# Attention scores, value sums and norm of a mixer laid out by feature tile

## The chip, the cores and the metric

The kernel runs on one core of a Trainium2 chip. The metric is the device time in microseconds (us) of one execution. Three runs of the kernel before gave a median of 1655.06 us (1654.47 to 1655.62). In the text PE is the matrix engine, DVE the vector engine, ACT the scalar engine, POOL is GpSimd and SP issues the weight transfers.

## The reference

One token block of 256 positions with 1024 features goes through a feed-forward layer, a hybrid mixer, a cross-attention, a second feed-forward layer and then a second block. All is fp32. The change lies in the hybrid mixer, in the part that the reference calls stick-breaking attention (16 heads of 64 features) and in the RMS norm of its result:

```python
z = jnp.einsum('bhtd,bhsd->bhts', qb, kb) * scale
causal = s_idx[None, :] < t_idx[:, None]
log_1mb = jnp.where(causal, jax.nn.log_sigmoid(-z), 0.0)
suffix = lax.cumsum(log_1mb, axis=3, reverse=True) - log_1mb
log_a = jnp.where(causal, jax.nn.log_sigmoid(z) + suffix, -jnp.inf)
a = jnp.exp(log_a)
outs.append(jnp.einsum('bhts,bhsd->bhtd', a, vb))
...
o_att = rmsnorm(o_att, attn_norm_g)          # over the 1024 features of a token
...
return jnp.concatenate([o_att, o_ssd], axis=-1) @ w_out
```

So each head needs scores, a masked exponential of running sums, a product with the values, and then one mean of squares over all 16 heads for each token.

## The kernel before, in words

Weights stream from HBM in units of 128 x 1024 fp32. For each unit SP loads one of three `raw` buffers, ACT rounds it to `hi` (L169), and DVE computes the remainder `lo = raw - hi` (L170). The next load into a `raw` buffer waits for the L170 that read it last. PE multiplies `hi` and `lo` with the activations, which stand in the same two parts (`uT`, `memT`), in three products. `f_tile` (L324) makes one tile of 128 output features by 256 tokens from one unit, 24 matmuls into one of two accumulators `mm`; an `evac` then copies the accumulator to SBUF, and the tile after the next can't start before that copy is done. `half_chunk` (L286) does the same token-major from four units.

Work that is not a weight product is written as Python generators ("sides"). `tick` is called at places in these loops with an estimate of time passed, and steps the sides that are due; a side yields the time after which it wants to go on. So the program order on each engine is fixed when the kernel is built, and each engine runs its instructions in that order, waiting on semaphores.

In the mixer, 8 pairs of f_tiles make `qT` and `kT` (feature-major: 128 features, two heads, to a tile). Two attention sides (`par` 0 and 1) run beside these and beside the 12 convolution tiles (`xs`, `bc`). A step of a side does two heads from two neighbouring feature tiles, both on the same 64 rows: scores (L612, L614), mask (L616, L617), ACT and DVE work, running sums (L634, L635, L637), exponentials and the product with the values (L647 to L649), whose result `oat` is token-major. There are 8 steps.

After the convolution tiles come the `z` product (two chunks of two halves, `half_chunk`), then 8 f_tiles `mk`, whose evacuation is a DVE copy (L933). The side `chain` (L898) is stepped within `z` and `mk`: squares of `oat` with row sums on ACT, `halves_rstd` (a DVE sum and a power of -1/2 on POOL, L438, for one column), the activation of the convolution result (L904), the scaling of `oat` on DVE (L910), and 16 PE transposes (L410 in `transposes`) that bring it feature-major into `oT`, rounded by ACT (L415) and DVE (L419) into two parts, with the gain per feature.

Of the kernel before, what the change touches and what calls it, by code (L numbers as in the profile page):

```python
# [5 lines left out]
F32 = mybir.dt.float32  # L6
# [5 lines left out]
AF = mybir.ActivationFunctionType  # L12
OP = mybir.AluOpType
# [3 lines left out]
EPS = 1e-6  # L17
# [43 lines left out]
COL = {}  # L61
# [55 lines left out]
class Builder:  # L117
# [475 lines left out]
    AW = (0.94, 1.2, 4.0, 4.0, 3.21)  # L593
    A0 = 12.35

    def attention(self, par, qT, kT, vt, oat, ready):

        nc = self.nc
        rows = slice(par * 64, par * 64 + 64)
        A, B = self.acc[2 * par], self.acc[2 * par + 1]  # L600
        z0, z1, o = A, B[:, 0:256], B[:, 256:512]
        zv, z1v = A.rearrange("p (n t) -> p n t", n=2), z1.rearrange("p (n t) -> p n t", n=2)
        ov = o.rearrange("p (t n c) -> p t n c", t=2, n=2)
        neg = self.neg_le[:, None, :].to_broadcast([128, 2, 128])
        oview = oat.rearrange("p t (j n q c) -> p t j n q c", j=4, n=2, q=2)
        opt = dict(skip_group_check=True)
        for j in range(4):
            while ready[0] <= j:
                yield
            for n in range(2):  # L610
                f = 2 * j + n
                nc.tensor.matmul(zv[:, n], kT[rows, f, 0:128], qT[rows, f, :], start=(n == 0), stop=False,  # L612
                                 **opt)
                nc.tensor.matmul(z1v[:, n], kT[rows, f, 128:256], qT[rows, f, 128:256], start=(n == 0),  # L614
                                 stop=False, **opt)
            nc.tensor.matmul(zv[:, :, 0:128], self.ident_bf, neg, start=False, stop=False, **opt)  # L616
            nc.tensor.matmul(z1v, self.ident_bf, neg, start=False, stop=False, **opt)  # L617
            sp = self.FA.alloc(768)
            s0, s1 = sp.ap[:, 0:512], sp.ap[:, 512:768]
            nc.scalar.activation(s0, z0, AF.Abs)  # L620
            nc.scalar.activation(s1, z1, AF.Abs)
            yield self.AW[0]
            nc.scalar.activation(sp.ap, sp.ap, AF.Exp, scale=-1.0)
            nc.scalar.activation(sp.ap, sp.ap, AF.Ln, bias=1.0)
            yield self.AW[1]
            nc.vector.scalar_tensor_tensor(s0, z0, 0.0, s0, op0=OP.max, op1=OP.add)
            nc.vector.scalar_tensor_tensor(s1, z1, 0.0, s1, op0=OP.max, op1=OP.add)
            ph, pl = self.RA.alloc(768), self.RA.alloc(768)
            nc.scalar.activation(ph.ap, sp.ap, AF.Copy)
            nc.vector.tensor_sub(pl.ap, sp.ap, ph.ap.bitcast(F32))  # L630
            yield self.AW[2]
            for p in (ph, pl):
                x0, x1 = p.ap[:, 0:512], p.ap[:, 512:768]
                nc.tensor.matmul(z0, self.ntri, x0, start=False, stop=False, **opt)  # L634
                nc.tensor.matmul(zv[:, :, 128:256], self.none, x1.rearrange("p (n t) -> p n t", n=2),  # L635
                                 start=False, stop=False, **opt)
                nc.tensor.matmul(z1, self.ntri, x1, start=False, stop=(p is pl), **opt)  # L637
            nc.scalar.activation(s0, z0, AF.Exp)
            nc.scalar.activation(s1, z1, AF.Exp)
            ph.free()  # L640
            pl.free()
            yield self.AW[3]
            for n in range(2):
                h = 4 * j + 2 * n + par
                vh = slice(h * 64, h * 64 + 64)
                a0, a1 = s0[:, n * 256:n * 256 + 256], s1[:, n * 128:n * 128 + 128]
                nc.tensor.matmul(ov[:, 0, n], a0[:, 0:128], vt[:, 0, vh], start=(n == 0), stop=False, **opt)  # L647
                nc.tensor.matmul(ov[:, 1, n], a0[:, 128:256], vt[:, 0, vh], start=False, stop=False, **opt)
                nc.tensor.matmul(ov[:, 1, n], a1, vt[:, 1, vh], start=False, stop=(n == 1), **opt)  # L649
            for n in range(2):  # L650
                nc.vector.tensor_copy(oview[:, :, j, n, par, :], ov[:, :, n])
            sp.free()
            yield self.AW[4]
        ready[1] += 1

# [181 lines left out]
    def mixer(self, before_t1, done, mid):  # L837
        nc, F, uT = self.nc, self.FA, self.uT
# [4 lines left out]
        vt = vb.v(t=2, d=1024)  # L843
# [2 lines left out]
            return lambda t, ps: nc.scalar.activation(vt[:, t, c * 512:c * 512 + 512], ps, AF.Copy)  # L846
        self.opening(FIRST["v"], uT, [evv(0), evv(1)], before_t1)
        mblocks, memT = self.tpair(8)
        qb, kb, ob = (F.alloc(2048) for _ in range(3))
        qT, kT, oat = qb.v(f=8, t=256), kb.v(f=8, t=256), ob.v(t=2, d=1024)  # L850
        nc.scalar.preload_act_table_set("natural_log_exp_and_others")
        self.add_side(self.mem_prep(memb, memT), 0.15)
        ready = [0, 0]
        for par in range(2):
            self.add_side(self.attention(par, qT, kT, vt, oat, ready), 0.2)[2] = par * self.A0
        for f in range(8):
            self.f_tile(FIRST["qk"] + 2 * f, uT,
                        lambda ps: nc.scalar.activation(qT[:, f], ps, AF.Copy, scale=0.125))
# [31 lines left out]
        oblocks, oT = self.tpair(8)  # L890
        kmb, zb = F.alloc(2048), F.alloc(2048)
        kmT, zt = kmb.v(f=8, t=256), zb.v(t=2, d=1024)
        ready = [0, 0, 0]
# [2 lines left out]
            return lambda t, ps: nc.scalar.activation(zt[:, t, c * 512:c * 512 + 512], ps, AF.Copy)  # L896

        def chain():  # L898
            rs = []
            for t in range(2):  # L900
                rs.append(self.halves_rstd(self.x_ss(oat[:, t])))
                yield 5.0
            for f in range(12):
                nc.scalar.activation(xp[:, f, 3:259], xp[:, f, 3:259], AF.Silu,  # L904
                                     bias=self.cols[:, COL["conv_b"] + f:COL["conv_b"] + f + 1])
                if f % 2:
                    yield 2.5
                if f in (3, 5):
                    t = f // 2 - 1
                    nc.vector.tensor_scalar(oat[:, t], oat[:, t], rs[t], None, op0=OP.mult)  # L910
                if f > 7:
                    n = f - 8
                    self.transposes(oat[:, n // 2], n // 2, oT, COL["attn_norm_g"], part=n % 2)
                    yield 0.3
            ob.free()
            ready[1] = 1
            nc.scalar.preload_act_table_set("natural_log_exp_and_others")
            yield from self.ssd(xp, zt, uT, ready)

        def gate():  # L920
# [4 lines left out]
            yield  # L925
        row = self.load_row("mix_post_g")
        self.add_side(chain(), 1.41)
        for c in range(2):
            self.tok_chunk(FIRST["z"] + 4 * c, uT, evz(c))
# [881 lines left out]
```

## Time and profile before

| what | value |
|---|---|
| profiled execution | 1655.53 us |
| its span in the trace | 1653.8 us |
| median of three runs | 1655.06 us |
| PE busy | 1632.5 us (99%) |
| DVE busy | 1148.0 us (69%) |
| ACT busy | 977.9 us (59%) |
| POOL busy | 268.6 us (16%) |

A busy time is the union of an engine's instructions. The profiled execution is 0.47 us above the median, and 1.7 us of it lie outside the span. In a timeline a row stands for one instruction or for several neighbours of one kind ("x2"), with its start and length in us; where the engine sat idle before it, brackets tell how long and what ended that. The chip runs an fp32 matmul as two passes, so one call of the program shows as two instructions; a matmul on fp32r operands is one. Matmuls overlap in their ends, so the cost of one in a dense stretch is the distance between starts, not its length.

### The profile page before, as it was taken

The page shows a single profiled execution, that of the slowest core. Times are in us where ns is not written, and L with a number is a line of the kernel's source. Part 1 is how long each engine was busy: PE and PEld are TensorE (multiplying, and loading weights), DVE is VectorE, ACT ScalarE, POOL GpSimd, SP SyncE. Part 2 cuts the span into 40 slices and gives each one's busy share as a digit, 9 for nine tenths or more (in the row PEclk, how much of TensorE's full clock was granted, in tenths as well). Part 3 has the DMA queues.
Part 4 walks back from the last instruction along what each step waited for, and adds up shares of the span by engine and source line. Part 5 has one row for each costly group of instructions (what it writes and reads, how often), then busy time and mean ns, then how long its engine had stood idle before and what let it go on. Part 6 is the DMA issues. An engine that isn't in the chain of part 4 may idle for free.

```text
span 1653.8 us, 29236 instructions
## 1 busy us (share of the span) xinstructions
PE 1632.5 (99%) x11102; PEld 1481.6 (90%) x11102; DVE 1148.0 (69%) x2366; ACT 977.9 (59%) x1826; POOL 268.6 (16%) x311
## 2 busy tenths in 40 slices
PE   8999999999999999999999999999999999999998
PEld 6999899988898899979889999999999888888886
DVE  6554765877756645487657998899999755555554
ACT  6443676786555544467355565888877555444454
POOL 0000000000000000000100003988888000000000
PEclk9999999999999999999999999999999999999999
DMA  7565643364524656555244555444454555555553
GB/s 280 192 208 175 227 143 116 115 202 143 179 103 154 216 190 206 177 185 197 78 140 143 192 190 192 166 163 164 161 166 153 180 205 194 194 195 193 191 191 128
DMA packets 79325, 288.77 MB, mean 175 GB/s; under 512 B 8784, under 2 KB 8912, under 8 KB 79056
## 3 DMA queue, kind: packets, MB, share of 16 engines
q1 hardware_dynamic: 77904, 281.66, 49.8%
q10 hardware_dynamic: 1280, 5.24, 1.0%
q8 instruction: 87, 1.43, 0.3%
q14 instruction: 54, 0.44, 0.1%
HBM read 285.82 MB, written 1.05 MB: 173 GB/s over the span
## 4 chain that ended last, share of the span: by engine, by line
PE 81%; DVE 11%; ACT 3%; issue 2%; DMA 2%; POOL 1%; SPq 0%; POOLq 0%; DVEq 0%; ACTq 0%
PE mm L332 12%; PE mm L334 12%; PE mm L333 12%; PE acc L349 10%; PE acc L351 10%; PE acc L353 10%; DVE lo L170 4%; PE mm L303 2%; PE mm L300 2%; PE mm L299 2%; DMA raw<-ws 2%; PE sd L1388 1%; ACT hi L169 1%; DVE m L1378 1%; DVE X L1260 1%
## 5 line engine op out<-in xcount | busy, mean ns | idle before, releaser
L170 DVE TENSOR_TENSOR lo<-raw,hi 128x1024 fp32r<-128x1024 f32 x414 | 506.6, 1228 | 237.5 <-ACT hi L169 236.1
L332 PE MATMUL mm<-uT,hi 128*128 128x256 f32 x2104 | 597.1, 284 | 2.1 <-DVE X L1491 1.7
L334 PE MATMUL mm<-uT,lo 128*128 128x256 f32 x2104 | 587.1, 279 | 0.0
L333 PE MATMUL mm<-uT,hi 128*128 128x256 f32 x2104 | 586.9, 279 | 0.0
L169 ACT ACTIVATE hi<-raw 128x1024 fp32r<-128x1024 f32 x414 | 436.3, 1058 | 214.9 <-PE acc L353 171.1
L332 PEld LDWEIGHTS mm<-uT,hi 128*128 128x128 f32 x2104 | 397.1, 189 | 4.9 <-DVE X L1491 2.6
L333 PEld LDWEIGHTS mm<-uT,hi 128*128 128x128 f32 x2104 | 397.1, 189 | 0.8
L334 PEld LDWEIGHTS mm<-uT,lo 128*128 128x128 f32 x2104 | 397.0, 189 | 0.0
L1375 POOL TENSOR_SCALAR m<-iota,kT 128x128 f16<-128x128 f16 x256 | 233.2, 927 | 197.8 <-DVE kT L1358 149.9
L438 POOL TENSOR_TENSOR hr<-hv,mhalf 128x1 f32<-128x1 f32 x26 | 14.4, 552 | 816.3 <-DVE hv L437 816.3
L349 PE MATMUL acc<-hi,wf 128*128 128x512 f32 x384 | 118.9, 390 | 0.0
L351 PE MATMUL acc<-lo,wf 128*128 128x512 f32 x384 | 118.7, 389 | 0.0
L353 PE MATMUL acc<-hi,wf 128*128 128x512 f32 x384 | 118.5, 389 | 0.0
L170 DVE TENSOR_TENSOR lo<-fa,hi 128x1024 fp32r<-128x1024 f32 x69 | 84.1, 1233 | 34.0 <-ACT hi L169 33.7
L531 ACT ACTIVATE fa<-mm 128x256 f32<-128x256 f32 x36 | 13.8, 383 | 122.9 <-PE mm L334 122.9
L351 PEld LDWEIGHTS acc<-lo,wf 128*128 128x128 f32 x384 | 72.1, 188 | 15.2
L353 PEld LDWEIGHTS acc<-hi,wf 128*128 128x128 f32 x384 | 72.1, 188 | 15.1
L349 PEld LDWEIGHTS acc<-hi,wf 128*128 128x128 f32 x384 | 72.1, 188 | 14.9
L1488 ACT ACTIVATE X<-mm 128x256 f32<-128x256 f32 (+40 forms) x126 | 39.6, 314 | 76.0 <-PE mm L334 75.0
L1377 ACT ACTIVATE oh<-m,kT 128x128 f16<-128x128 f16 x256 | 81.1, 390 | 0.0
L169 ACT ACTIVATE hi<-fa 128x1024 fp32r<-128x1024 f32 x69 | 70.7, 1051 | 5.6 <-PE mm L303 3.1
L1398 DVE TENSOR_TENSOR X<-sd,X 128x184 f32<-128x184 f32 (+31 forms) x64 | 60.9, 951 | 1.2 <-ACT X L1396 1.1
(364 smaller groups left out, 2550.9 us busy)
## 6 DMA issues: line engine op xcount, KB each, us to landing
raw<-ws SPq DMA_DIRECT2D x442, 512.0 KB, 3.3
fa<-ws SPq DMA_DIRECT2D x91, 512.0 KB, 4.4
fa<-rows ACTq DMA_DIRECT2D x5, 512.0 KB, 4.7
fa<-mem ACTq DMA_DIRECT2D x1, 1024.0 KB, 7.7
X<-keysT ACTq DMA_DIRECT2D x1, 1024.0 KB, 5.0
out<-X SPq DMA_DIRECT2D x4, 256.0 KB, 2.0
h<-x SPq DMA_DIRECT2D x2, 256.0 KB, 2.8
h<-x SPq DMA_DIRECT2D x1, 512.0 KB, 7.3
```

The source lines that it names most:

```text
L169: nc.scalar.activation(hi, raw, AF.Copy)
L170: nc.vector.tensor_sub(lo, raw, hi.bitcast(F32))
L332: nc.tensor.matmul(ps, wh, ah[:, k, :], start=(k == 0), stop=False)
L333: nc.tensor.matmul(ps, wh, al[:, k, :], start=False, stop=False)
L334: nc.tensor.matmul(ps, wl, ah[:, k, :], start=False, stop=(k == 7))
L349: nc.tensor.matmul(o[h], ah[:, k, ts], hi[:, hs[h]], start=first, stop=False)
L351: nc.tensor.matmul(o[h], ah[:, k, ts], lo[:, hs[h]], start=False, stop=False)
L353: nc.tensor.matmul(o[h], al[:, k, ts], hi[:, hs[h]], start=False, stop=last)
L1375: nc.gpsimd.tensor_scalar(m1[:, i], self.iota, key(0, i), None, op0=OP.is_equal)
L1377: nc.scalar.activation(oh[:, i], m1[:, i], AF.Copy, scale=key(2, i))
L1398: nc.vector.tensor_mul(x[:, :, 0:E], pv[:, :, 0:E], x[:, :, 0:E])
L1488: nc.scalar.activation(X[:, i, g:256], ps[:, g:256], AF.Gelu)
```

## The change

A step of the attention now does the two heads of one feature tile: head n uses rows 64n to 64n+63 of the array for its scores and has an accumulator bank of its own (`zb[n]`). The value product is turned round: the values are the stationary operand, the result comes feature-major, head n in output partitions 64n to 64n+63 (the array's columns, `tile_position`), and one DVE copy puts it into `oA`. POOL squares it (L650, L652) and adds up the squares of the 8 tiles (L653). In `chain` one matmul with a matrix of ones (L901) sums the squares over the features and leaves the sum of each token in all partitions; DVE scales it and adds the epsilon (L903), POOL raises the 128 x 256 result to -1/2 (L904), DVE multiplies `oA` by it in two halves (L913), and ACT (L917) and DVE (L918) make the two parts of `oT` with the gain. The squares on ACT, the two powers of one column and the 16 transposes of `oat` are gone.

```diff
-    def attention(self, par, qT, kT, vt, oat, ready):
+    def attention(self, par, qT, kT, vt, oT, sq, ready):
...
+            for c, ts, ks in ((slice(0, 256), slice(0, 256), slice(0, 128)),
+                              (slice(256, 384), slice(128, 256), slice(128, 256))):
+                for n in range(2):
+                    rows = slice(64 * n, 64 * n + 64)
+                    nc.tensor.matmul(zb[n][:, c], kT[rows, f, ks], qT[rows, f, ts], start=(ks.start == 0), stop=False,
+                                     **opt)
...
             for p in (ph, pl):
-                x0, x1 = p.ap[:, 0:512], p.ap[:, 512:768]
-                nc.tensor.matmul(z0, self.ntri, x0, start=False, stop=False, **opt)
-                nc.tensor.matmul(zv[:, :, 128:256], self.none, x1.rearrange("p (n t) -> p n t", n=2),
-                                 start=False, stop=False, **opt)
-                nc.tensor.matmul(z1, self.ntri, x1, start=False, stop=(p is pl), **opt)
...
+                for n in range(2):
+                    x = tri(p.ap, n)
+                    nc.tensor.matmul(zb[n][:, 0:384], self.ntri, x, start=False, stop=False, **opt)
+                    nc.tensor.matmul(zb[n][:, 128:256], self.none, x[:, 256:384], start=False, stop=(p is pl), **opt)
...
-                nc.tensor.matmul(ov[:, 0, n], a0[:, 0:128], vt[:, 0, vh], start=(n == 0), stop=False, **opt)
-                nc.tensor.matmul(ov[:, 1, n], a0[:, 128:256], vt[:, 0, vh], start=False, stop=False, **opt)
-                nc.tensor.matmul(ov[:, 1, n], a1, vt[:, 1, vh], start=False, stop=(n == 1), **opt)
...
+            for k, ts, a in ((0, slice(0, 256), slice(0, 256)), (1, slice(128, 256), slice(256, 384))):
+                for n in range(2):
+                    h = 2 * f + n
+                    nc.tensor.matmul(o[64 * n:64 * n + 64, ts], vt[:, k, h * 64:h * 64 + 64], tri(sp.ap, n)[:, a],
+                                     start=(k == 0), stop=(k == 1), tile_position=(0, 64 * n), **opt)
+            nc.vector.tensor_copy(oT[:, f], o)
...
+                nc.gpsimd.tensor_tensor(sq[:, 1], oT[:, f], oT[:, f], op=OP.mult)
+                nc.gpsimd.tensor_tensor(sq[:, 0], sq[:, 0], sq[:, 1], op=OP.add)
...
         def chain():
-            rs = []
-            for t in range(2):
-                rs.append(self.halves_rstd(self.x_ss(oat[:, t])))
-                yield 5.0
+            ps = self.sd()
+            nc.tensor.matmul(ps[:, 0:256], self.ones, sq[:, 0], start=True, stop=True)
+            v, r = sq[:, 1], sq[:, 0]
+            nc.vector.tensor_scalar(v, ps[:, 0:256], 1.0 / 1024, EPS, op0=OP.mult, op1=OP.add)
+            nc.gpsimd.tensor_tensor(r, v, self.mhalf[:, 0:1].to_broadcast([128, 256]), op=OP.pow)
+            yield 10.0
...
                 if f in (3, 5):
-                    t = f // 2 - 1
-                    nc.vector.tensor_scalar(oat[:, t], oat[:, t], rs[t], None, op0=OP.mult)
+                    half = oA[:, 2 * f - 6:2 * f - 2]
+                    nc.vector.tensor_tensor(half, half, r[:, None, :].to_broadcast([128, 4, 256]), op=OP.mult)
                 if f > 7:
-                    n = f - 8
-                    self.transposes(oat[:, n // 2], n // 2, oT, COL["attn_norm_g"], part=n % 2)
+                    for k in (2 * f - 16, 2 * f - 15):
+                        gain = self.cols[:, COL["attn_norm_g"] + k:COL["attn_norm_g"] + k + 1]
+                        nc.scalar.activation(oT[0][:, k], oA[:, k], AF.Copy, scale=gain)
+                        nc.vector.scalar_tensor_tensor(oT[1][:, k], oA[:, k], gain, oT[0][:, k].bitcast(F32),
+                                                       op0=OP.mult, op1=OP.subtract)
```

The first piece of order is PE's, the scores and the mask of the first step (`acc` are the accumulator banks, `fa` holds qT and kT); rows with - are of the kernel before, rows with + of the changed one.

```order
 L612 MATMUL acc_71<-fa 128x256
-L614 MATMUL acc_72<-fa 128x128
-L612 MATMUL acc_71<-fa 128x256
-L614 MATMUL acc_72<-fa 128x128
-L616 LDWEIGHTS identb
-L616 MATMUL acc_71<-negle,identb 128x2x128
-L617 LDWEIGHTS identb
-L617 MATMUL acc_72<-negle,identb 128x256
+L612 MATMUL acc_72<-fa 128x256
+L612 MATMUL acc_71<-fa 128x128
+L612 MATMUL acc_72<-fa 128x128
```

The same four matmuls go out, now alternating between the two halves of the rows and between two banks; the two masks (128 x 256 each) stay.

The second piece is POOL's, from the last steps of the attention to the chain; the long run of L399 and L438 rows is the one-column powers.

```order
+L684 MEMSET part 96x256
+L652 TENSOR_TENSOR fa<-fa 128x256
+L653 TENSOR_TENSOR fa<-fa 128x256
+L652 TENSOR_TENSOR fa<-fa 128x256
+L653 TENSOR_TENSOR fa<-fa 128x256
+L904 TENSOR_TENSOR fa<-fa,mhalf 128x256
+L736 TENSOR_TENSOR fa<-fa,dec 128x1024
 L399 TENSOR_TENSOR rr<-rv,mhalf 128x1 x4
```

POOL gets two products a step, and one power on 128 x 256 (L904), before what it did already.

The third piece is DVE's, during `z` (`lo`, `hi` and `raw` with the numbers of their buffers; the `L170` rows prepare the units of `mk`).

```order
+L903 TENSOR_SCALAR fa<-sd_76 128x256
 L170 TENSOR_TENSOR lo_82<-raw_79,hi_81 128x1024
 L170 TENSOR_TENSOR lo_107<-raw_80,hi_106 128x1024
 L170 TENSOR_TENSOR lo_105<-raw_78,hi_104 128x1024
 L170 TENSOR_TENSOR lo_103<-raw_79,hi_102 128x1024
-L910 TENSOR_SCALAR fa<-fa,hr 128x1024
-L170 TENSOR_TENSOR lo_89<-raw_80,hi_88 128x1024
-L910 TENSOR_SCALAR fa<-fa,hr 128x1024
+L913 TENSOR_TENSOR fa<-fa 128x1024
+L170 TENSOR_TENSOR lo_89<-raw_80,hi_88 128x1024
+L913 TENSOR_TENSOR fa<-fa 128x1024
 L170 TENSOR_TENSOR lo_100<-raw_78,hi_99 128x1024
```

L903 and the first L913 take the places of the two small sums and of L910. L913 waits for POOL's L904, and the next L170, of buffer 89, stands behind it; the unit of that L170 is the fifth of the eight `mk` tiles.

## Rows read from the trace of the kernel before

**Rows 1.** page: busy time and share; granted clock, 40 slices, in tenths.

```profile
PE 1632.5 (99%) x11102; PEld 1481.6 (90%) x11102; DVE 1148.0 (69%) x2366; ACT 977.9 (59%) x1826; POOL 268.6 (16%) x311
...
PEclk9999999999999999999999999999999999999999
```

**Rows 2.** busy us of each engine in a stretch of the mixer, PE first.

```profile
220.00:400.00 180.00, 179.74 (x1351) 168.81 (x1350) 120.50 (x200) 131.57 (x243) 4.98 (x8) 1.00 0.43 145
```

**Rows 3.** timeline of PE, first attention step, scores: start, length, what.

```profile
235.08 0.38 PE L614 MATMUL acc<-fa 64*128 64x128 f32 x2
235.30 0.59 PE L612 MATMUL acc<-fa 64*128 64x256 f32 x2
235.74 0.38 PE L614 MATMUL acc<-fa 64*128 64x128 f32 x2
```

**Rows 4.** timeline of PE, the same step, products with the values.

```profile
251.88 0.33 PE L647 MATMUL acc<-fa 128*128 128x64 f32 x2
...
253.14 0.36 PE L332 MATMUL mm<-uT,hi 128*128 128x256 f32 x1
```

**Rows 5.** timeline of PE, second block: products on parts of the array.

```profile
787.27 1.16 PE L1119 MATMUL sd<-fa 32*128 32x128 f32 x16
788.36 0.38 PE L332 MATMUL mm<-uT,hi 128*128 128x256 f32 x1
...
805.97 1.07 PE L1144 MATMUL acc<-fa 128*32 128x128 f32 x24
806.97 1.16 PE L1119 MATMUL sd<-fa 32*128 32x128 f32 x16
```

**Rows 6.** timeline of PE, the same step, running sums.

```profile
245.69 0.40 PE L634 MATMUL acc<-ra,ntri 128*128 128x512 f32 x1
245.93 0.28 PE L635 MATMUL acc<-ra,none 128*128 128x256 f32 x1
...
246.64 0.28 PE L332 MATMUL mm<-uT,hi 128*128 128x256 f32 x1
```

**Rows 7.** timeline of PE, transposes of oat, first and third mk tile.

```profile
359.59 0.60 PE L410 MATMUL sd<-ident,fa 128*128 128x128 f32 x4
359.94 0.37 PE L332 MATMUL mm<-ra,hi 128*128 128x256 f32 x1
...
366.96 0.36 PE L332 MATMUL mm<-ra,hi 128*128 128x256 f32 x1
```

**Rows 8.** POOL's powers, by line and shape: count, busy us, mean ns.

```profile
L438 POOL TENSOR_TENSOR hr<-hv,mhalf 128x1 f32<-128x1 f32 x26 | 14.4, 552 | 816.3 <-DVE hv L437 816.3
L399 POOL TENSOR_TENSOR rr<-rv,mhalf 128x4 f32<-128x4 f32 x6 | 6.1, 1009 | 87.8 <-DVE rv L398 87.8
```

**Rows 9.** timeline of DVE, from the z product into mk.

```profile
342.16 1.23 DVE L170 TENSOR_TENSOR lo<-raw,hi 128x1024 fp32r<-128x1024 f32 x1 [1.34 <-ACT hi L169]
...
353.73 0.75 DVE L910 TENSOR_SCALAR fa<-fa,hr 128x1024 f32<-128x1024 f32 x1
...
364.33 0.42 DVE L933 COPY fa<-mm 128x256 f32<-128x256 f32 x1
```

**Rows 10.** of the page: rounding, remainder and load of one unit.

```profile
L170 DVE TENSOR_TENSOR lo<-raw,hi 128x1024 fp32r<-128x1024 f32 x414 | 506.6, 1228 | 237.5 <-ACT hi L169 236.1
...
L169 ACT ACTIVATE hi<-raw 128x1024 fp32r<-128x1024 f32 x414 | 436.3, 1058 | 214.9 <-PE acc L353 171.1
...
raw<-ws SPq DMA_DIRECT2D x442, 512.0 KB, 3.3
```

**Rows 11.** timelines of POOL and DVE, where they meet, at two places.

```profile
112.79 3.07 POOL L429 TENSOR_SCALAR fa<-fa 128x1024 f32<-128x1024 f32 x1 [98.31 <-DMA fa<-rows]
...
113.62 1.56 DVE L170 TENSOR_TENSOR lo<-fa,hi 128x1024 fp32r<-128x1024 f32 x1
...
373.66 1.91 POOL L735 TENSOR_TENSOR fa<-fa,dec 128x1024 f32<-128x1024 f32 x1 [27.43 <-DVE fa L721]
...
374.03 2.62 DVE L170 TENSOR_TENSOR lo<-raw,hi 128x1024 fp32r<-128x1024 f32 x1
```

More of the change, by code (lines that the diff above doesn't have):

```diff
@@ L594 @@
     A0 = 12.35
-    def attention(self, par, qT, kT, vt, oat, ready):
+    def attention(self, par, qT, kT, vt, oT, sq, ready):
         nc = self.nc
[L599 to L603, printed above, removed]
+        zb = [self.acc[2 * par], self.acc[2 * par + 1]]
+        o = zb[0][:, 0:256]
@@ L604, in attention @@
         neg = self.neg_le[:, None, :].to_broadcast([128, 2, 128])
-        oview = oat.rearrange("p t (j n q c) -> p t j n q c", j=4, n=2, q=2)
         opt = dict(skip_group_check=True)
-        for j in range(4):
-            while ready[0] <= j:
+        tri = lambda ap, n: ap[:, 384 * n:384 * n + 384]
+        for f in range(par, 8, 2):
+            while ready[0] <= f // 2:
                 yield
-            for n in range(2):
[L611 to L621, printed above, removed]
+            for c, ts, ks in ((slice(0, 256), slice(0, 256), slice(0, 128)),
[4 more added lines that the diff above has]
+                                     **opt)
+            for z in zb:
+                nc.tensor.matmul(z.rearrange("p (c t) -> p c t", c=2)[:, :, 0:128], self.ident_bf, neg, start=False,
+                                 stop=False, **opt)
+            sp = self.FA.alloc(768)
+            for n in range(2):
+                nc.scalar.activation(tri(sp.ap, n), zb[n][:, 0:384], AF.Abs)
@@ L625, in attention @@
             yield self.AW[1]
-            nc.vector.scalar_tensor_tensor(s0, z0, 0.0, s0, op0=OP.max, op1=OP.add)
-            nc.vector.scalar_tensor_tensor(s1, z1, 0.0, s1, op0=OP.max, op1=OP.add)
+            for n in range(2):
+                nc.vector.scalar_tensor_tensor(tri(sp.ap, n), zb[n][:, 0:384], 0.0, tri(sp.ap, n), op0=OP.max,
+                                               op1=OP.add)
             ph, pl = self.RA.alloc(768), self.RA.alloc(768)
@@ L632, in attention @@
             for p in (ph, pl):
-                x0, x1 = p.ap[:, 0:512], p.ap[:, 512:768]
-                nc.tensor.matmul(z0, self.ntri, x0, start=False, stop=False, **opt)
-                nc.tensor.matmul(zv[:, :, 128:256], self.none, x1.rearrange("p (n t) -> p n t", n=2),
-                                 start=False, stop=False, **opt)
-                nc.tensor.matmul(z1, self.ntri, x1, start=False, stop=(p is pl), **opt)
-            nc.scalar.activation(s0, z0, AF.Exp)
-            nc.scalar.activation(s1, z1, AF.Exp)
+                for n in range(2):
+                    x = tri(p.ap, n)
+                    nc.tensor.matmul(zb[n][:, 0:384], self.ntri, x, start=False, stop=False, **opt)
+                    nc.tensor.matmul(zb[n][:, 128:256], self.none, x[:, 256:384], start=False, stop=(p is pl), **opt)
+            for n in range(2):
+                nc.scalar.activation(tri(sp.ap, n), zb[n][:, 0:384], AF.Exp)
             ph.free()
@@ L642, in attention @@
             yield self.AW[3]
[L643 to L646, printed above, removed]
-                nc.tensor.matmul(ov[:, 0, n], a0[:, 0:128], vt[:, 0, vh], start=(n == 0), stop=False, **opt)
-                nc.tensor.matmul(ov[:, 1, n], a0[:, 128:256], vt[:, 0, vh], start=False, stop=False, **opt)
-                nc.tensor.matmul(ov[:, 1, n], a1, vt[:, 1, vh], start=False, stop=(n == 1), **opt)
-            for n in range(2):
-                nc.vector.tensor_copy(oview[:, :, j, n, par, :], ov[:, :, n])
-            sp.free()
+            for k, ts, a in ((0, slice(0, 256), slice(0, 256)), (1, slice(128, 256), slice(256, 384))):
+                for n in range(2):
+                    h = 2 * f + n
+                    nc.tensor.matmul(o[64 * n:64 * n + 64, ts], vt[:, k, h * 64:h * 64 + 64], tri(sp.ap, n)[:, a],
+                                     start=(k == 0), stop=(k == 1), tile_position=(0, 64 * n), **opt)
+            nc.vector.tensor_copy(oT[:, f], o)
+            sp.free()
+            if not ready[2]:
+                ready[2] = 1
+                nc.gpsimd.tensor_tensor(sq[:, 0], oT[:, f], oT[:, f], op=OP.mult)
+            else:
+                nc.gpsimd.tensor_tensor(sq[:, 1], oT[:, f], oT[:, f], op=OP.mult)
+                nc.gpsimd.tensor_tensor(sq[:, 0], sq[:, 0], sq[:, 1], op=OP.add)
             yield self.AW[4]
@@ L848, in mixer @@
         mblocks, memT = self.tpair(8)
-        qb, kb, ob = (F.alloc(2048) for _ in range(3))
-        qT, kT, oat = qb.v(f=8, t=256), kb.v(f=8, t=256), ob.v(t=2, d=1024)
+        qb, kb, ob, sqb = (F.alloc(n) for n in (2048, 2048, 2048, 512))
+        qT, kT, oA, sq = qb.v(f=8, t=256), kb.v(f=8, t=256), ob.v(f=8, t=256), sqb.v(i=2, t=256)
         nc.scalar.preload_act_table_set("natural_log_exp_and_others")
         self.add_side(self.mem_prep(memb, memT), 0.15)
-        ready = [0, 0]
+        ready = [0, 0, 0]
         for par in range(2):
-            self.add_side(self.attention(par, qT, kT, vt, oat, ready), 0.2)[2] = par * self.A0
+            self.add_side(self.attention(par, qT, kT, vt, oA, sq, ready), 0.2)[2] = par * self.A0
         for f in range(8):
@@ L908, in chain @@
                 if f in (3, 5):
-                    t = f // 2 - 1
-                    nc.vector.tensor_scalar(oat[:, t], oat[:, t], rs[t], None, op0=OP.mult)
+                    half = oA[:, 2 * f - 6:2 * f - 2]
+                    nc.vector.tensor_tensor(half, half, r[:, None, :].to_broadcast([128, 4, 256]), op=OP.mult)
                 if f > 7:
-                    n = f - 8
-                    self.transposes(oat[:, n // 2], n // 2, oT, COL["attn_norm_g"], part=n % 2)
+                    for k in (2 * f - 16, 2 * f - 15):
[3 more added lines that the diff above has]
+                                                       op0=OP.mult, op1=OP.subtract)
                     yield 0.3
             ob.free()
+            sqb.free()
             ready[1] = 1
```

## The prediction

> **What bounds the kernel now.** I read the page's busy times first: PE is busy for 99% of the span, DVE for 69%, and the granted clock is full in all 40 slices [rows 1]. Then the windows over the stretch of the mixer that the change touches: from 220 to 400 us PE works 179.74 of 180 us, while DVE has 59 and ACT 48 us to spare [rows 2]. So here a microsecond taken from PE shortens the kernel by a microsecond, and work of DVE, ACT and POOL is free until PE has to wait for it. Then the timeline of PE at the pieces that are edited, that of DVE behind them, and the group rows of POOL.
>
> **The change part by part.** *Scores.* Two passes of a 128-column fp32 matmul take 235.30 - 235.08 = 0.22 us, two of a 256-column one 235.74 - 235.30 = 0.44 us [rows 3]. A step has two of each, one after another, as all use the same 64 rows. Do two matmuls on different rows run at once? In the second block 16 passes of 128 columns that alternate between row groups take 788.36 - 787.27 = 1.09 us with the entry and the exit, where 16 single ones would take 16 x 0.11 = 1.76 us [rows 3, 5]; inside, a pair costs what one costs. So each step saves one of each size, 0.66 us, and 8 steps 5.3 us. The ends are nothing (no overlap) and 5.3 us; I take 5.3.
>
> *Product with the values.* Before: six matmuls of 64 columns, 253.14 - 251.88 = 1.26 us [rows 4]. Now: two of 256 and two of 128 columns, in pairs on the two column halves. 24 passes on three column groups take 806.97 - 805.97 = 1.00 us against 24 x 0.11 = 2.6 us for single ones [rows 3, 5], so column parts overlap too. A step is then 0.44 + 0.22 = 0.66 us, and about 0.2 us for changing into and out of the parts (787.27 to 788.36 is 1.09 us for 8 pairs of 0.11 = 0.88). It saves 1.26 - 0.86 = 0.40 us, 3.2 us in 8 steps; without overlap it would lose 0.26 us a step, 2.1 us in all.
>
> *Running sums.* Before, two matmuls of 512 columns and four of 256 take 246.64 - 245.69 = 0.95 us, and one of 512 takes 0.24 us [rows 6]. Now there are four of 384 columns (0.24 x 384/512 = 0.18 us) and four of 128. No row has a small fp32r matmul. Its bounds are 0.06 us (a quarter of 0.24) and 0.22 us (two fp32 passes); I take one fp32 pass, 0.11 us [rows 3]. That is 4 x 0.29 = 1.16 us, 0.21 us more in a step and 1.7 us in 8, with bounds of 0 and 5.2 us. The attention together: 5.3 + 3.2 - 1.7 = 6.8 us less on PE.
>
> *Norm on PE.* Four groups of transposes go, 359.94 - 359.59 = 0.35 us each [rows 7], 1.4 us. One 256-column fp32 product with ones comes, 0.44 us and a little for the change of type, 0.5 us. PE alone would save 6.8 + 1.4 - 0.5 = 7.7 us.
>
> *Copies, ACT and DVE.* The Abs, Exp and copy work of a step keeps its number of elements; the squares on ACT go; 16 roundings of 128 columns become 8 of 256. The spare time above hides all of it, and I put it at nothing. If that cover were gone, the two L913 would cost what an L170 costs, 1.2 us each [rows 10].
>
> *The squares on POOL.* 15 instructions of 128 x 256, about a quarter of L735's 1.91 us each [rows 11]. They come right behind DVE's copy of the tile, where DVE's convolution work goes on, and rows 11 show an L170 that met L735 held from 374.03 for 2.62 us instead of 1.23. Bounds: 0, and 15 x 0.5 = 7 us of DVE. Only where convolution tiles run beside the last steps is DVE close to its limit; I take 1 us.
>
> *The power on POOL, the term that decides.* The same operation, a fp32 power with two tensor operands, takes 552 ns on 128x1 and 1009 ns on 128x4 [rows 8]: each further column adds (1009 - 552) / 3 = 152 ns. For 256 columns this is 0.55 + 255 x 0.152 = 39.4 us. The bounds of the unknown: 0.6 us (further columns cost nothing beyond a multiplication's 1.91 us / 1024 = 1.9 ns) and 256/4 x 1.009 = 65 us. I take 39.4, the line through the only two rows of this operation.
>
> The Trainium skill, page "GPSIMD Engine Reference", section "Performance versus the Vector engine", says that GpSimd's elementwise instructions cost about 2.6 cycles for an element and core, whatever the count. The multiplication agrees (1.9 ns a column [rows 11]); the power's 152 ns a column doesn't [rows 8]. By the page the power would be done in about 1 us; that is a rival below.
>
> *What waits for it.* When does it start, and when does PE need it? The sum of squares comes after the first unit of `z`; DVE's L903 stands behind the L170 of 342.16, which ends at 343.39 [rows 9]. With 0.42 us for a 128x256 result out of an accumulator (the L933 row [rows 9]), the power could start at 343.8 on the clock of the kernel before, and at 343.8 - 6.8 = 337.0 with the shorter attention. It ends at 337.0 + 39.4 = 376.4. DVE gets to L913 where L910 stood, at 353.7 - 6.8 = 346.9 [rows 9], and waits for 29.5 us. Behind it stand the remainders of the units of `mk` 4 to 7, and the copy that empties the accumulator of `mk` 0. `mk` 2 writes that accumulator, so PE stops there. Without a wait PE would reach `mk` 2 at 366.96 - 7.7 = 359.3 [rows 7]. With it: L913, L170, L913, L170, L170 (5 x 1.23 = 6.2 us, all as an L170), two L918 (0.8 us, as two L933), the L170 of `mk` 7 and the copy (1.23 + 0.42 us), together 8.6 us. The `raw` buffer of `mk` 7 is free after the second of them, at 2.5 us, loaded at 5.8 and rounded at 6.9 us [rows 10], just in time. PE goes on at 376.4 + 8.6 = 385.0, after 26 us of idling, and 385.0 - 366.96 = 18.0 us later than before. From there PE has the work it had, and nothing is given back.
>
> *Sum.* 1655.5 (the profiled execution) + 18.0 + 1 = 1674.5 us. The profiled execution is 0.5 us over the median, so I predict 1674. The clock after such a pause has no row here; I put it at nothing, and the range has room for it.
>
> **Rivals.** *DVE is held from the start of the power.* L735, with two tensor operands like the power, held an L170 until it was done [rows 11]. If L904 does so for its whole 39 us, DVE stops ten microseconds sooner, with the remainders of all eight `mk` units undone. After the power come three L170, then a wait for the fourth's `raw` buffer (1.2 + 3.3 + 1.06 = 5.6 us [rows 10]) and the rest in the same way; the copy is done some 15 us after the power instead of 8.6, which gives 1681 us. Against it: L429 ran from 112.79 to 115.86, and an L170 begun at 113.62 took 1.56 us and ended well before it [rows 11].
>
> The Trainium skill, page "SBUF — State Buffer", section "Who interferes with whom", says that a DVE instruction with two SBUF inputs and a GpSimd instruction that reads SBUF exclude each other for the whole of the earlier one. The pair at 374.03 agrees, the pair at 113.62 doesn't [rows 11]: it was lengthened by 0.3 us, not held. By the page the time is 1681; by the second pair it is the forecast.
>
> *The power is cheap per column* (the other side). If POOL works off a wide operand in another way than four columns, L904 takes less. PE doesn't wait if 337.0 + P + 8.6 is under 359.3, that is up to P = 14 us; then only the PE terms count, 1655.5 - 7.7 = 1648 us. From P = 20 us on (337.0 + P + 8.6 + 1 = 366.96) the kernel is slower. For it: the 552 ns of one column hold some 400 ns that don't grow. Against it: three more columns cost three times the same, and nothing in 1009 ns looks shared. P between 14 and 30 us gives 1648 to 1665.
>
> *The pairs don't overlap.* Then scores save nothing, values lose 2.1 and sums 1.7 us, and the wait stays: 1674 + 6.8 + 3.8 = 1685 us. Rows 5 speak against it.
>
> **How the numbers follow.** Forecast 0.42; DVE held throughout 0.25; no overlap 0.04; cheap power 0.17; P in between 0.12, two thirds of it over 20 us. A difference under 0.2% (3.3 us) can't be told from no change here. Slower by more: 0.42 + 0.25 + 0.04 + 0.07 = 0.78; within: 0.04; faster: 0.17 and a little of the middle, 0.18. The forecast's own range is 1667 to 1680. The range of 1655 to 1690 takes in DVE held throughout, a steeper power and most of the middle, and leaves out the cheap power.
>
> **What would show it.** Right: in the trace after, one POOL instruction at L904 of about 39 us; DVE idle before L913 with POOL as releaser; PE idle for some 26 us before the third `mk` tile, with DVE's copy as releaser. Scores with starts in pairs, and 0.66 us less a step. An L170 of 20 us or more during L904 would show the first rival; a short L904 with no gap on PE the second. The forecast is wrong if L904 takes under 20 us, or if PE finds the accumulator of `mk` 0 empty.

## The result and the profile after

The changed kernel takes 1680.24 us (median of 4 runs, 1679.06 to 1681.9), the one before 1655.34 (1654.47 to 1656.08) beside it: ratio 1.015, 95% interval 1.0137 to 1.0162. The prediction was 1674 with a range of 1655 to 1690, so it held in direction, mechanism and range, and was 6 us short. The profiled execution took 1680.41 us with a span of 1678.7.

From the page: busy times, then the granted clock and POOL in 40 slices (before: [rows 1]).

```profile
PE 1626.7 (97%) x11072; PEld 1473.9 (88%) x11072; DVE 1147.4 (68%) x2349; ACT 973.3 (58%) x1810; POOL 325.5 (19%) x325
...
POOL 0000001181000000000110002888888100000000
PEclk9999999987999999999999999999999999999999
```

PE has 6 us less work than before and yet the kernel is longer: the work went, and idle time came. Slices 8 and 9 of POOL read 8 and 1 (counted from 0), slices 8 and 9 of the clock 8 and 7. So the place is near 340 to 400 us. The same stretch as [rows 2], then three pieces of it (busy us of PE, PEld, DVE, ACT, POOL, then the granted clock):

```profile
220.00:400.00 180.00, 149.99 (x1138) 138.87 (x1137) 106.54 (x161) 110.42 (x197) 57.63 (x20) 0.91 0.38 128
...
360.00:375.00 15.00, 0.25 (x3) 0.05 (x1) 0.00 (x0) 0.00 (x0) 15.00 (x1) 0.64 0.00 0
375.00:390.00 15.00, 0.25 (x1) 0.25 (x2) 8.42 (x10) 4.26 (x9) 6.29 (x1) 0.50 0.29 88
390.00:400.00 10.00, 10.00 (x65) 9.81 (x66) 8.62 (x16) 6.00 (x9) 0.00 (x0) 0.76 0.75 235
```

From 360 to 375 us only POOL works. The clock column (third from the right) shows a second loss: while PE stood, the granted clock fell to 0.50, which is the level of 1.2 GHz, and over the first 10 us of work behind the pause it was 0.76 on average. The timelines name the instructions; POOL first, then DVE, then PE (start, length, what, idle time before it and its releaser):

```profile
340.14 41.15 POOL L904 TENSOR_TENSOR fa<-fa,mhalf 128x256 f32<-128x256 f32 x1 [11.35 <-DVE fa L903]
```

```profile
338.50 1.23 DVE L170 TENSOR_TENSOR lo<-raw,hi 128x1024 fp32r<-128x1024 f32 x1 [1.34 <-ACT hi L169]
...
340.45 2.62 DVE L170 TENSOR_TENSOR lo<-raw,hi 128x1024 fp32r<-128x1024 f32 x2 [0.38 <-ACT hi L169]
...
349.02 1.22 DVE L170 TENSOR_TENSOR lo<-raw,hi 128x1024 fp32r<-128x1024 f32 x1 [2.43 <-ACT hi L169]
381.33 1.23 DVE L913 TENSOR_TENSOR fa<-fa 128x1024 f32<-128x1024 f32 x1 [31.08 <-POOL fa L904]
...
389.28 0.42 DVE L940 COPY fa<-mm 128x256 f32<-128x256 f32 x1
```

```profile
389.75 0.58 PE L332 MATMUL mm<-ra,hi 128*128 128x256 f32 x1 [29.50 <-DVE fa L940]
```

One chain, read backwards: PE waits 29.5 us for the copy of the accumulator (L940), that copy stands on DVE behind L913, and L913 waits 31.1 us for the power. PE is at `mk` 2 at 389.75 instead of 366.96 [rows 7], 22.8 us later. From there to the end of the span it is 1678.7 - 389.75 = 1288.95 us against 1653.8 - 366.96 = 1286.84 before: 2.1 us more, about what 10 us at 0.76 lose (2.4 us). It is all lost close behind the pause: 8 us on, at the third group of four transposes from `mk` 2 on, the changed kernel is at 397.48 and the one before at 372.64, 24.84 us apart. 22.8 + 2.1 = 24.9 us is the whole difference of the two spans.

What the change meant to save is there too. Timeline of PE, first step: scores and mask, sums, values (before: [rows 3, 4, 6]).

```profile
234.64 0.92 PE L612 MATMUL acc<-fa 64*128 64x256 f32 x8
235.50 0.39 PE L615 MATMUL acc<-negle,identb 128*128 128x256 bf16 x2
...
244.49 0.34 PE L634 MATMUL acc<-ra,ntri 128*128 128x384 f32 x1
...
245.59 0.33 PE L332 MATMUL mm<-uT,hi 128*128 128x256 f32 x1
...
251.18 0.87 PE L644 MATMUL acc<-fa 128*64 128x256 f32 x8
251.98 0.39 PE L332 MATMUL mm<-uT,hi 128*128 128x256 f32 x1
```

And the scores of before, of which [rows 3] hold the middle:

```profile
234.55 0.70 PE L612 MATMUL acc<-fa 64*128 64x256 f32 x2
...
236.05 0.28 PE L616 MATMUL acc<-negle,identb 128*128 128x256 bf16 x1
```

From the first score to the mask it is 235.50 - 234.64 = 0.86 us, before 236.05 - 234.55 = 1.50; the sums take 245.59 - 244.49 = 1.10 us (0.95 before), the values 0.80 us (1.26 before). Getting into the column parts costs a little more: 0.21 us pass from the last product ahead of the values to the first of them, 0.12 before.

### The profile page after: what moved, and what is told of

It reads as the page before. It is cut to its first block, busy times and chain, and to the rows that moved or that the text cites. A ratio compares the mean times of both kernels' runs of the same rounds, so it can differ in the third digit from the quotient of the medians.

```text
span 1678.7 us, 29154 instructions
## 1 busy us (share of the span) xinstructions
PE 1626.7 (97%) x11072; PEld 1473.9 (88%) x11072; DVE 1147.4 (68%) x2349; ACT 973.3 (58%) x1810; POOL 325.5 (19%) x325
## 3 DMA queue, kind: packets, MB, share of 16 engines
q8 instruction: 86, 1.41, 0.3%
## 4 chain that ended last, share of the span: by engine, by line
PE 82%; DVE 7%; ACT 3%; POOL 3%; issue 3%; DMA 2%; SPq 0%; POOLq 0%; ACTq 0%; DVEq 0%
PE mm L332 14%; PE mm L334 13%; PE mm L333 13%; PE acc L349 10%; PE acc L351 10%; PE acc L353 10%; DVE lo L170 3%; POOL fa L904 2%; PE mm L303 2%; PE mm L300 2%; PE mm L299 2%; PE sd L1395 1%; DMA raw<-ws 1%; ACT hi L169 1%; ACT junk L443 1%
## 5 line engine op out<-in xcount | busy, mean ns | idle before, releaser
L170 DVE TENSOR_TENSOR lo<-raw,hi 128x1024 fp32r<-128x1024 f32 x414 | 504.9, 1224 | 238.6 <-ACT hi L169 237.3
L438 POOL TENSOR_TENSOR hr<-hv,mhalf 128x1 f32<-128x1 f32 x24 | 13.2, 549 | 722.7 <-DVE hv L437 722.7
L170 DVE TENSOR_TENSOR lo<-fa,hi 128x1024 fp32r<-128x1024 f32 x69 | 83.9, 1230 | 34.0 <-ACT hi L169 33.7
```

What stands on the lines that cost most here:

```text
L170: nc.vector.tensor_sub(lo, raw, hi.bitcast(F32))
```

## The experiments

Ten kernels ran, each beside the kernel before (1655.39 to 1656.02 us). Theory A is the prediction's: what costs is DVE waiting in order for a power of 41 us. The main rival B says that the new layout or its work on POOL costs the time.

**e1_mult: a product in place of the power.**

```diff
-nc.gpsimd.tensor_tensor(r, v, self.mhalf[:, 0:1].to_broadcast([128, 256]), op=OP.pow)
+nc.gpsimd.tensor_tensor(r, v, self.mhalf[:, 0:1].to_broadcast([128, 256]), op=OP.mult)
```

> The power of the 128x256 tile becomes a product of the same two operands on the same engine; the scale that the norm multiplies by is left out of the output. Theory A (the power's length is the whole loss): the instruction falls from 41.15 us to about 1.5 us (a product of this shape took 0.72 to 1.68 us), VectorE goes on at 350, its last copy lands at about 358.6, before TensorE comes to mk2 at 360.25, and the 29.5 us wait and the some 2 us of low clock behind it go: 1680.2 - 31.6 = 1648.6 us. Rival B (the new layout of attention, its GpSimd products or the new waits in it cost the time, and the power lies beside something as long): at least 1665 us.

1650.09 us, ratio to before 0.9969 (0.9957 to 0.998). POOL's timeline in it:

```profile
340.52 0.61 POOL L904 TENSOR_TENSOR fa<-fa,mhalf 128x256 f32<-128x256 f32 x1 [11.35 <-DVE fa L903]
```

The same place, shape and operands, 0.61 us instead of 41.15, and the kernel is 30.1 us shorter than the changed one. B falls: the layout itself wins 5.3 us. It is 1.5 us over what was expected; PE now waits 1.03 us for DVE at L718, a wait that the changed kernel did not have.

**e2_half_power and e10_quarter_power: the power of 128 and of 64 columns, the rest a product.**

```diff
-nc.gpsimd.tensor_tensor(r, v, self.mhalf[:, 0:1].to_broadcast([128, 256]), op=OP.pow)
+nc.gpsimd.tensor_tensor(r[:, 0:128], v[:, 0:128], self.mhalf[:, 0:1].to_broadcast([128, 128]), op=OP.pow)
+nc.gpsimd.tensor_tensor(r[:, 128:256], v[:, 128:256], self.mhalf[:, 0:1].to_broadcast([128, 128]), op=OP.mult)
```

(e10: 0:64 and 64:256.)

> The power is taken of 128 of the 256 columns, the other 128 get a product (half of the tokens are scaled wrongly). Theory A with a price per column (41.15 us / 256 = 0.16 us): power 20.6 us, product 0.8 us, VectorE released at about 361.6, copies done 370.0, TensorE waits about 10 us instead of 29.5: 1658 to 1660 us. Rival B1 (the power has a price per instruction, not per column): wait stays near 29 us, 1680 us. Rival B2 (price grows faster than the columns): wait under 5 us, under 1654 us.

> As e2, with the power of 64 of the 256 columns and a product for the other 192 (three quarters of the tokens are scaled wrongly). By the price per column of the two powers so far (41.15 us for 256, 20.75 us for 128: 0.159 us a column and 0.35 us) it takes 10.5 us, from 340.5 to 351.0. VectorE is ready for the result at about 350.3. Theory: no wait of TensorE, 1650 to 1651 us as with a product of the whole tile. Rival (a power of any length keeps a part of the loss, by the port or by what stands behind it): 1653 to 1656 us.

1660.8 us, ratio 1.0033 (1.0022 to 1.0044), and 1651.04 us, ratio 0.9965 (0.9952 to 0.9979). POOL's two rows and PE's wait in e2, then POOL's power in e10:

```profile
341.03 20.75 POOL L904 TENSOR_TENSOR fa<-fa,mhalf 128x128 f32<-128x128 f32 x1 [11.35 <-DVE fa L903]
361.75 0.40 POOL L905 TENSOR_TENSOR fa<-fa,mhalf 128x128 f32<-128x128 f32 x1
...
370.67 0.58 PE L332 MATMUL mm<-ra,hi 128*128 128x256 f32 x1 [9.53 <-DVE fa L942]
```

```profile
340.08 10.54 POOL L904 TENSOR_TENSOR fa<-fa,mhalf 128x64 f32<-128x64 f32 x1 [11.35 <-DVE fa L903]
```

The power is a straight line from 64 to 256 columns: (41.15 - 10.54) / 192 = 0.159 us a column, and 0.34 us. Half of it leaves 9.5 us of PE's wait, and the kernel is 10.7 us over e1 (0.8 us over what was expected); the quarter makes DVE wait 1.06 us and PE not at all at `mk` 2, and the time is e1's. (PE's one wait there is 2.7 us at L718, behind DVE's wait for the d_skip row; e9 is on that.) So the loss is the part of the power that sticks out of PE's cover, and the rivals of e2 and e10 fall.

**e4_narrow: the power of 128x2.** The sums are taken token by token, and two products with the identity spread the result over the columns.

```diff
-nc.tensor.matmul(ps[:, 0:256], self.ones, sq[:, 0], start=True, stop=True)
-... (L902 to L904: scale, power of 128x256)
-yield 10.0
+for t in range(2):
+    nc.tensor.matmul(ps[:, t:t + 1], sq[:, 0, t * 128:t * 128 + 128], self.ones[:, 0:1], start=True, stop=True)
+c = self.rstd(ps[:, 0:2], 1024, 2)
+yield 5.0
+ps = self.sd()
+for t in range(2):
+    nc.tensor.matmul(ps[:, t * 128:t * 128 + 128], c[:, t:t + 1].to_broadcast([128, 128]), self.ident, start=True,
+                     stop=True)
+r = sq[:, 1]
+nc.vector.tensor_copy(r, ps[:, 0:256])
+yield 5.0
```

> As the run before without the power that nobody reads: the whole reference is computed, with the power of 128x2 instead of 128x256. Theory A: power about 0.7 us (128x1 took 0.55, 128x4 1.01), no wait at mk2; the new small products of TensorE add under 1 us: 1649 us (1647.5 to 1651), so 6 us below the kernel before. Rival B (layout or GpSimd products cost the time): at least 1665 us. Against the run before it: equal within 2 us by theory A, over 20 us shorter by rival C, 5 to 20 us shorter by rival D.

1654.74 us, ratio 0.9997 (0.9987 to 1.0006): 25.5 us under the changed kernel, but almost 6 us over what was expected. POOL and PE there, then the window behind the wait:

```profile
339.67 0.72 POOL L399 TENSOR_TENSOR rr<-rv,mhalf 128x2 f32<-128x2 f32 x1 [11.08 <-DVE rv L398]
...
340.44 1.22 PE L908 MATMUL sd<-ident,rr 128*128 128x128 f32 x4 [2.72 <-POOL rr L399]
```

```profile
341.00:344.00 3.00, 3.00 (x11) 2.47 (x10) 0.42 (x1) 0.00 (x0) 0.00 (x0) 0.54 0.38 139
```

The power is 0.72 us, but I had put its reader on PE too early: PE waits 2.72 us for it, and in the 3 us behind that wait the granted clock is 0.54, so even a short pause costs again. That is the expectation's miss, and the next run's edit.

**e5_late_spread: the spreading products 4 us later** (pauses of 9.0 and 1.0 instead of 5.0 and 5.0).

```diff
 c = self.rstd(ps[:, 0:2], 1024, 2)
-yield 5.0
+yield 9.0
...
 nc.vector.tensor_copy(r, ps[:, 0:256])
-yield 5.0
+yield 1.0
```

> As the narrow power (e4), with the products that spread the scale over the columns put 4 us later in the side's schedule (pauses of 9 and 1 instead of 5 and 5). In e4 TensorE waited 2.7 us at them for GpSimd's power and went at half pace for some 2 us behind the wait. Theory: both go, 2.7 + 1.0 to 1.3 us: 1651 us (1650 to 1652), within 1 us of the kernel with a product in place of the power (1650.1). Rival: the small products, the copy and the second use of the score buffer cost the 4.6 us themselves: 1653 us or more.

1650.65 us, ratio 0.9967 (0.9955 to 0.998), as expected: the wait at L908 is gone and the clock reads 1.00 in that window. With that it beats both kernels, the one before by 0.3%.

**e3_unread: e4 with the wide power beside it, of a tile that nobody reads.**

```diff
+nc.vector.tensor_copy(self.dead, ps[:, 0:256])
+nc.gpsimd.tensor_tensor(self.dead, self.dead, self.mhalf[:, 0:1].to_broadcast([128, 256]), op=OP.pow)
 nc.vector.tensor_copy(r, ps[:, 0:256])
```

> Sums token by token: two products with one column of ones give 128x2 sums, the power is taken of 128x2, and two products with the identity spread it over the columns again. Beside that the power of a 128x256 tile stays in the program right behind it on GpSimd, of a tile that nothing else reads. Theory A (what costs is that VectorE waits in order for the power, not that GpSimd runs it): the power takes 41 us from about 346 to 387, VectorE and TensorE don't wait for it, 1649 to 1651 us. Rival C (GpSimd's power slows or holds VectorE through the port they share): 1670 us or more. Rival D (GpSimd's own queue: the product of line 736 and the SSD's small powers come up to 20 us later behind it): TensorE waits behind the first half of wo1, 1655 to 1670 us.

1662.8 us, ratio 1.0046 (1.003 to 1.0063), 8.1 us over e4: rival D. POOL, what waits for it on PE, and one of DVE's L170 meanwhile:

```profile
341.69 41.14 POOL L912 TENSOR_TENSOR dead<-dead,mhalf 128x256 f32<-128x256 f32 x1 [1.31 <-DVE dead L911]
382.80 1.90 POOL L736 TENSOR_TENSOR fa<-fa,dec 128x1024 f32<-128x1024 f32 x1
...
384.75 3.78 PE L742 MATMUL sd<-fa 128*128 128x512 f32 x4 [4.99 <-POOL fa L736]
...
348.00 1.23 DVE L170 TENSOR_TENSOR lo<-raw,hi 128x1024 fp32r<-128x1024 f32 x1 [0.16 <-ACT hi L169]
```

All 13 of DVE's L170 inside this power take 1.22 to 1.23 us, so rival C (a port held by it) falls a second time. But POOL's own queue matters, and theory A of this run falls too: L736, the next product in that queue, starts at 382.80 instead of 377.82 (e4), PE waits 5.0 us for it, and L742 behind that wait takes 3.78 us instead of 1.98 (e5), at a granted clock of 0.50 from 384 to 388 us. So the power costs 30.1 us where DVE waits for it (the changed kernel against e1) and 8.1 us where nobody reads it (e3 against e4). The 8.1 us are the longer wait (4.99 us instead of 0.21), the slow L742 (1.8 us), some 0.5 us in the next 4 us at a clock of 0.87, and 1 us that I did not trace.

**e6_no_products: the 14 products and sums of the squares on POOL left out** (the `else` branch at L651 to L653).

> As e5, but only the first feature tile's squares are taken: the 14 other products and sums on GpSimd are left out, so the norm divides by one tile's mean square instead of all eight. Theory (their contention with VectorE is real but lies beside TensorE's work): VectorE's L878 and L880 go back from about 545 to about 480 ns, time within 1 us of e5. Rival (contention reaches TensorE through the evictions of attention): 2 to 3 us shorter than e5.

1649.75 us, ratio 0.9962 (0.9948 to 0.9975): not told apart from e5. DVE's convolution rows by line, of e5 and then of e6 (count, busy us, mean ns):

```profile
L878 DVE SCALAR_TENSOR_TENSOR fa<-fa,cols 128x256 f32<-128x256 f32 x24 | 13.1, 544 | 1.1 <-ACT fa L876 0.7
L880 DVE SCALAR_TENSOR_TENSOR fa<-fa,cols 128x256 f32<-128x256 f32 x12 | 6.6, 546 | 0.4
```

```profile
L875 DVE SCALAR_TENSOR_TENSOR fa<-fa,cols 128x256 f32<-128x256 f32 x24 | 11.5, 481 | 1.1 <-ACT fa L873 0.7
L877 DVE SCALAR_TENSOR_TENSOR fa<-fa,cols 128x256 f32<-128x256 f32 x12 | 5.8, 486 | 0.4
```

The timeline of DVE in e6, ahead of the norm:

```profile
336.18 1.23 DVE L170 TENSOR_TENSOR lo<-raw,hi 128x1024 fp32r<-128x1024 f32 x1 [1.34 <-ACT hi L169]
```

The products lengthen DVE's work by 13.1 + 6.6 - 11.5 - 5.8 = 2.4 us, and the L170 ahead of the norm comes at 336.18 instead of the 338.50 of the changed kernel (338.59 in e5). In the changed kernel those 2.3 us moved the start of the power. With a short power most of it is covered, but not all: in the changed kernel and in e5 PE waits twice, 0.5 us together, for the sums of the eighth and last step, and in e6 it doesn't. The changed kernel's PE:

```profile
314.03 0.44 PE L634 MATMUL acc<-ra,ntri 128*128 128x384 f32 x1 [0.30 <-ACT ra L628]
...
315.02 0.44 PE L634 MATMUL acc<-ra,ntri 128*128 128x384 f32 x1 [0.21 <-DVE ra L629]
```

So the rival has a grain of truth, of a size (0.9 us between the medians of e5 and e6) that these runs can't tell from nothing.

**e7_unpaired: both products of head 0, then both of head 1**, in the scores and in the values.

```diff
-for c, ts, ks in (...):
-    for n in range(2):
+for n in range(2):
+    for c, ts, ks in (...):
```

> As e5, with the four score products and the four value products of a step issued one half of the array after the other (both of head 0, then both of head 1) instead of alternating; the same products, the same halves. Theory (halves overlap only when the next instruction uses the other half): only the middle two can overlap, a step loses 0.3 to 0.65 us on the scores and 0.15 to 0.35 us on the values, in 8 steps +4 to +8 us: 1655 to 1659 us. Rival (they overlap in any order, or the gain of the layout is the fewer columns alone): same as e5 within 1 us.

1650.81 us, ratio 0.9968 (0.9956 to 0.998). My theory falls. PE's first step in it:

```profile
234.56 0.93 PE L612 MATMUL acc<-fa 64*128 64x256 f32 x8
235.42 0.39 PE L615 MATMUL acc<-negle,identb 128*128 128x256 bf16 x2
```

0.86 us from the first score to the mask, as in pairs; the values, on the two halves of the columns, take 0.81 us (0.80 in pairs). The two halves of the array ran side by side although all four passes of one half stood ahead of the other's in the program; the alternation buys nothing.

**e8_act_squares: the squares by ScalarE out of PSUM**, the sums still on POOL.

```diff
-nc.gpsimd.tensor_tensor(sq[:, 1], oT[:, f], oT[:, f], op=OP.mult)
+nc.scalar.activation(sq[:, 1], o, AF.Square)
```

> As e5, with the eight squares taken by ScalarE from PSUM instead of by GpSimd from the copy; the seven sums stay on GpSimd. Computes the whole reference. It takes 8 x 0.4 us to ScalarE, which is busy 71% of the attention's second half, and takes half of GpSimd's products away. Theory (neither engine is on the path there): 1650.5 to 1652 us, VectorE's L878 at about 510 ns. Rival (ScalarE's chain of Abs, Exp, Ln is what TensorE waits for): 1653 to 1656 us.

1655.88 us, ratio 1.0003 (0.9993 to 1.0012): the rival. PE's waits from 252 to 333 us (total, times, longest):

```profile
PE mm L332 <- ACT fa L873: 2.2, 3, 1.2
PE acc L634 <- ACT ra L628: 1.0, 1, 1.0
```

ScalarE was 71% busy there in e5 (56.94 of 80 us from 252 to 332), and yet PE now waits 3.2 us for it (0.3 us in e5). ACT's timeline in e8, then PE's, show why:

```profile
330.28 0.38 ACT L652 ACTIVATE fa<-acc 128x256 f32<-128x256 f32 x1 [2.18 <-DVE fa L646]
330.56 0.38 ACT L873 ACTIVATE fa<-mm 128x256 f32<-128x256 f32 x1
...
330.99 0.38 PE L332 MATMUL mm<-uT,hi 128*128 128x256 f32 x1 [1.24 <-ACT fa L873]
```

The square (L652) itself is short, but it waits 2.18 us for DVE's copy of the same tile (L646), and L873, the eviction that PE needs, stands behind it in ACT's queue. It is the mechanism of the changed kernel in the small: an instruction that waits in order holds what stands behind it. DVE's L878 took 482 ns and not the 510 that I expected. POOL was the better engine.

**e9_early_row: e5 with the d_skip row loaded some 15 us earlier.**

```diff
+dsk = self.load_row("d_skip")
 for f in range(12):
...
-yield from self.ssd(xp, zt, uT, ready)
+yield from self.ssd(xp, zt, uT, ready, dsk)
```

> As e5, with the load of the d_skip row issued some 15 us earlier, at the start of the side that computes the norm instead of at the start of the SSD. In the profiles of the kernels without the long wait, VectorE's L724 waits 0.2 to 1.9 us for that row and TensorE 0.8 to 2.6 us behind it at L718. Theory (TensorE's earlier arrival is partly taken back there): the wait at L718 for L724 falls to 0.3 us or less, 0.5 to 2 us less than e5: 1649 to 1650 us. Rival (the wait is covered, or moves to the next product of the SSD): 1650.5 us as e5.

1650.98 us, ratio 0.9971 (0.9959 to 0.9982): no difference from e5 that can be told. The wait itself shrank, from 0.8 us in e5's profile to 0.4 us, and its cause, DVE's wait for the row, is gone. Whether 0.4 us reached the end is below what these runs resolve.

## Why the prediction was right, and where it was short

*Power.* Forecast 39.4 us by a line through one and four columns, measured 41.15; the line's slope of 152 ns was 159. Right. By the Trainium skill's page "GPSIMD Engine Reference", section "Performance versus the Vector engine", it would have been about 1 us, an estimate from its 2.6 cycles an element; the trace disagrees for the power (41.15 us) and agrees for the product of the same shape (0.61 us).

*Start of the power.* This is the term that was most off: 340.14 instead of 337.0. Two causes: the prediction let DVE come earlier by all of PE's 6.8 us, and it costed the squares on POOL at 1 us at the end of the sum instead of ahead of the power. Without the 14 products and sums (e6) DVE's L170 is at 336.18 and not at 335.4 (342.16 - 6.8), which is 0.8 us; no run shows why, but in e6 DVE runs without a gap from 329 to 334.8 us, so its own pace may count there and not PE's. With them it is 2.3 us later still. 0.8 + 2.3 = 3.1.

*What waits.* Right in each link: DVE at L913, the copy at its end, `mk` 2 on PE. From the start of L913 to the end of the copy 8.6 us were forecast, and it is 8.4 (381.33 to 389.70). PE came to `mk` 2 at 389.75 - 29.50 = 360.25, forecast 359.3, and went on at 389.75, forecast 385.0: 3.1 us from the start of the power and 1.75 from its length, less 0.1.

*The clock after the pause.* Put at nothing, measured 2.1 us. The sum closes: the forecast of 1674.5, 4.75 us later at `mk` 2, 1 us that was counted beside it for the squares and is now in it, and 2.1 for the clock, 1674.5 + 4.75 - 1 + 2.1 = 1680.35 against 1680.41. The median of 1680.24 us stands at the upper end of the forecast's own 1667 to 1680, inside the range of 1655 to 1690.

*PE's savings.* In the first step the scores save 1.50 - 0.86 = 0.64 us (forecast 0.66), the values take 0.80 us, 0.89 with the way into the column parts (forecast 0.86), the sums 1.10 (forecast 1.16). Net at `mk` 2: 7.7 forecast, 6.7 measured (366.96 - 360.25). The 1.0 us between them is at one place: the sums of the last step, with the two waits shown at e6, take about 1 us more than those of the first. In e1, where nothing waits for the power, PE comes to `mk` 2 at 360.46, 6.5 us earlier than before; at the third group of transposes behind it PE waits 1.03 us for DVE (L718), before 0.27 us, and 6.5 - 0.8 = 5.7 is the difference of the two profiled spans (1653.8 - 1648.1).

*Rivals.* DVE held by the port: refuted by the four L170 inside the power and by the 13 of e3. Three of the four took 1.22 to 1.23 us; the first, begun 0.3 us into the power, took 1.39, and 1.41 in e1, where a product of 0.61 us stands in its place. That it would have given 1681, near the measured 1680, is chance: only the trace tells the two apart. The rule of the Trainium skill's page "SBUF — State Buffer", section "Who interferes with whom", by which an instruction of DVE with two inputs in SBUF and one of POOL that reads SBUF exclude each other, is not borne out for the power (1.22 to 1.23 us for the 13 L170 of e3). The products did lengthen such operations of DVE: L878 took 544 ns beside them and 481 without (e6). Cheap power: refuted by 41.15 us. Of its break-even, no wait up to 14 us fits e10 (10.5 us, no wait at `mk` 2), but slower from 20 us on was too high: by that sum a power of 20.75 us should have cost 0.4 us, and e2 was 5.4 us slower than the kernel before (its power began at 341.03 and not 337.0, and PE's clock read 0.68 from 370 to 380 us). No overlap: refuted by the scores' 0.86 us.

## What to carry to other kernels

Price an operation by its own rows, at its own width: on the same engine and tile a product took 0.61 us and a power 41.15, and two small rows of the power predicted the wide one within 5%. A slow instruction on an engine with room still costs what sticks out between its operands and the first engine that waits for it in order, so do the slow step on the narrow form of the data (128x2) and widen it afterwards, and put the reader far enough behind it. When PE has been made faster, look again at which engine its next wait is for.

## What the runs showed of the hardware that was not expected

- A power on POOL costs 0.159 us a column of 128 fp32 values from 64 to 256 columns (10.54, 20.75, 41.15 us), in line with 0.55, 0.72 and 1.01 us for 1, 2 and 4 columns.
- Products on the two halves of PE's rows or columns overlap in both orders that were tried, also with four passes of one half ahead of the other's (e7: 0.86 us on the rows and 0.81 on the columns, in pairs 0.86 and 0.80).
- PE's granted clock fell to the lower of its levels after waits of 29.5, 5.0 and 2.7 us (0.50, 0.50 and 0.54 in the stretches behind or in them), and PE paid for it once work had come back: some 2 us behind the long wait, 1.8 us in L742 alone behind the 5 us.
